# The forward-substitution steps of a delta-rule layer, moved from VectorE to GpSimd

## The chip, the cores and the metric

One core of one Trainium2 chip runs the whole program in one launch. The metric is the device time of that launch in microseconds, the median of several runs; lower is better.

In the rows of the profile PE is TensorE (PEld its weight loads), DVE is VectorE, ACT is ScalarE, POOL is GpSimd and SP is SyncE, whose queue issues most of the DMAs. L657 is line 657 of the kernel; a tile is named without its buffer number.

## The reference

One layer of a decoder trunk on 512 positions of width 2048, in float32:

```
h = RMSNorm(x);  z = h @ w_in
RWKV half (16 heads of 64): token shift of r, k, v and two small projections;
    w = exp(-exp(-softplus(-(w0 + tanh(wd) @ w_up)) - 0.5));  a = sigmoid(a0 + ad @ a_up)
    kk = normalized k * k_k;  k = k * (1 + (a - 1) * k_a)
    per head, over t:  S = S * w_t + (S @ -kk_t) (kk_t * a_t) + v_t k_t^T;  y_t = S @ r_t
    group norm per head, plus sum(r * k * r_k) * v, times silu(gate)
Pool half (4 groups of 256): trailing means over 2, 4, 8, 16 positions minus the token,
    a linear map per group, a scale, times silu(gate)
x = x + concat(halves) @ w_out
x = x + sigmoid(x @ w_pg + b_pg) * (p @ w_ple);  out = RMSNorm(x)
```

The recurrence over t is not run token by token. The kernel cuts the 512 positions into 8 chunks of 64. Inside a chunk the delta rule is a triangular system, whose inverse is needed; from chunk to chunk only the 64 x 64 state of a head is handed on.

## The kernel before

Every large product is split into three fp32r matmuls (high x high, high x low, low x high), so each weight chunk of 256 KB that the SP queue loads (`raw_*`) is cast on ScalarE (`whi_*`, L132) and its remainder is taken on VectorE (`wlo_*`, L133). Four buffers of each kind rotate.

The RWKV half is worked through in 8 pairs of heads, `j` = 0 to 7. For one pair: `prepare` makes the scaled keys and queries, `scores(j)` the triangular matrices `mt`, `invert(j)` inverts their 32 x 32 diagonal blocks by forward substitution, `gather(j)` builds the rest of the inverse `x1` from them, and `recur(j)` runs the 8 chunks. The work of neighbouring pairs overlaps: after the first chunk of `recur(j)` come `scores(j + 1)`, and the substitution of pair j + 1 runs during the later chunks of `recur(j)`. Between all these TensorE is fed with the matmuls of the input projection (`zk`, `zr`, `zv`, `zg` and the pool columns `zb`), which `pump` hands out a few at a time; the order on TensorE in this stage is the order of the program text (`keep_in_program_order`). On the other engines a scheduler sets the order when the program is built; each engine then works through its own queue strictly in that order, and so does SP.

A chunk `ch` of `recur` is a chain of hops, each with some 6 to 9 matmuls of the projection behind it:

- TensorE `py` reads the state `sbd`; VectorE forms `zs` (L787);
- TensorE `pu` multiplies by `x1`; ScalarE copies it to `uv` (L797);
- TensorE `ps` makes the state's update; VectorE forms the next state `sbd` in two halves. In chunk 0 that is L807, in the chunks 1 to 6 L809, which adds `s0p`;
- GpSimd forms `s0p`, the new state times the next chunk's decay, in two halves (L816). The next chunk's L809 reads it.

So `s0p_2` (made after chunk 2) is read by L809 of chunk 3, `s0p_3` by that of chunk 4, and so on up to `s0p_5`.

`invert(j)` is a generator of 31 steps of two instructions each: L657 multiplies a column of the result so far (`xw`) by a row of the matrix (`n`, loaded twice over from DRAM) into `tm`, and L661 adds `tm` to `xw`. Each reads what the one ahead of it wrote, so the 62 form one chain. The shapes run from 31 columns over 76 to 8 columns, 1560 columns over the 31 steps. Behind the last step SP writes `xw` to DRAM (`xd`, L665, four DMAs) and reads it back in another layout into `x1` (L672, four DMAs); VectorE transposes half of it (L734), and the matmuls `pq` use that.

Before the change the steps ran on VectorE, and inside `recur` they were tied to the hops: from the sixth hop on, each hop's end asked for two steps, to be issued behind the VectorE instruction that the hop had just issued (`lead`). For pair 0, whose `invert(0)` runs ahead of all recurrences, nothing was tied.

```
HC, HT, HX = (6, 9, 9), 130, 13
HS, HN = 5, 2                      # from which hop on, steps per hop
for _ in invert(0): pass           # pair 0
recur(j, invert(j + 1) if j + 1 < NJ else iter(()), between)
```

Of the kernel before, what the change touches and what calls it, by code (L numbers as in the profile page):

```python
# [13 lines left out]
ALU = mybir.AluOpType  # L14

P = 128
# [18 lines left out]
def trunk_kernel(ctx: ExitStack, tc: tile.TileContext, x, p, norm_g, w_in, mu, w0, w_up, a0, a_up,  # L35
                 k_k, k_a, r_k, ln_w, ln_b, w_pool, pool_scale, w_out, w_ple, w_pg, b_pg, final_g, out):
    nc = tc.nc
# [155 lines left out]
    n_ = 0  # L193
# [456 lines left out]
    def invert(j):  # L650
        nb = st_[j].pop("nb")
        xw = rw.tile([P, 8, 32], F32, name=f"xw{j}", tag="xw")
        tm = rw.tile([P, 8, 32], F32, name=f"tm{j}", tag="tm")
        for s in range(31):
            n_, w_ = s // 4 + 1, 31 - s
            xin = i32 if s == 0 else xw
            nc.vector.tensor_tensor(tm[:, 0:n_, 0:w_], xin[:, 0:n_, s:s + 1].to_broadcast([P, n_, w_]),  # L657
                                    nb[s // 16][:, s % 16:s % 16 + 1, s + 1:32].to_broadcast([P, n_, w_]), ALU.mult)
            if s == 0:
                nc.gpsimd.tensor_copy(xw, i32)  # L660
            nc.vector.tensor_tensor(xw[:, 0:n_, s + 1:32], xw[:, 0:n_, s + 1:32], tm[:, 0:n_, 0:w_], ALU.add)  # L661
            yield
        xd = dram.tile([2, 2, 8, 8, 4, 32], F32, name=f"xd{j}", tag="xd")
        for q in range(4):
            nc.sync.dma_start(out=xd[:, :, :, :, q, :].rearrange("a b u i c -> (a b u) i c"),  # L665
                              in_=xw[32 * q:32 * q + 32])
        x1 = rw.tile([P, 8, C], F32, name=f"x1{j}", tag="x1", bufs=2)
        nc.gpsimd.memset(x1, 0.0)
        for par in range(2):
            pb = 64 * (1 - par)  # L670
            for b in range(2):
                nc.sync.dma_start(out=x1[pb + 32 * b:pb + 32 * b + 32, :, 32 * b:32 * b + 32],  # L672
                                  in_=xd[par, b].rearrange("u i q c -> (i q) u c"))

        st_[j]["x1"] = x1
# [80 lines left out]
    def recur(j, work, between):  # L756
# [4 lines left out]
        lead = [None]  # L761


        def step():
            hop[0] += 1
            if hop[0] > HS:
                with tc.issue_after(lead[0].ins):
                    for _ in range(HN):
                        next(work, None)


        ysb = rw.tile([P, NT, P], F32, name=f"ysb{j}", tag="t", bufs=4)
# [1 line left out]
        for ch in range(NCH):  # L774
# [8 lines left out]
            if ch > 0:  # L783
                mm(py[:, sl], ar[:, q, 2 * par:2 * par + 2, :], cur, start=ch in (1, 4), stop=True,
                                 skip_group_check=True)
                with tc.high_priority(offset=HP):
                    lead[0] = nc.vector.tensor_tensor(zs[pb:pb + 64], py[pb:pb + 64, sl], mv[pb:pb + 64, q, :],  # L787
                                                      ALU.add)
                step()
                pump(HC1)  # L790
# [3 lines left out]
            for h in range(2):  # L794
                hc = slice(64 * h, 64 * h + 64)
                with tc.high_priority(offset=HP):
                    nc.scalar.copy(uv[pb:pb + 64, ch, hc], psu[hc, hc])  # L797
            step()
            pump(HC2)
            if ch < NCH - 1:  # L800
# [16 lines left out]
            if ch % 4 == 3:  # L817
# [10 lines left out]
                for pr in range(2):  # L828
                    yr = slice(64 * pr, 64 * pr + 64)
                    nc.scalar.copy(ysb[yr, q - 1:q + 1, :], py4[yr, pr::2, :])  # L830
            step()
            if ch == 0:
                between()
# [37 lines left out]
    HS, HN = 5, 2  # L871
# [12 lines left out]
    for _ in invert(0):  # L884
        pass
    pump(HT)
    gather(0)
    for j in range(NJ):
        def between():
            pump(H3 if j + 1 < NJ else HC[2])  # L890
            if j + 1 < NJ:
                scores(j + 1)
                pump_to(H2)

        if j + 1 == NJ:
            pn.append(rw.tile([P, NT, DPLE], F32, name="pn", tag="ar", bufs=2))
            for h in range(2):
                nc.scalar.dma_start(out=pn[0][:, 2 * h:2 * h + 2, :],
                                    in_=p[256 * h:256 * h + 256, :].rearrange("(t p) q -> p t q", p=P))
        if j + 1 < NJ:  # L900
            prepare(j + 1)
        recur(j, invert(j + 1) if j + 1 < NJ else iter(()), between)
        if j + 1 < NJ:
            gather(j + 1)
# [276 lines left out]
```

## Time and profile before

| | us |
|---|---|
| median of 3 runs | 1099.41 (1097.35 to 1099.85) |
| span of the profiled execution | 1095.9 |
| PE busy | 1070.8 (98%) |
| DVE busy | 708.2 (65%) |
| ACT busy | 448.3 (41%) |
| POOL busy | 76.9 (7%) |

The profiled execution's span runs from its first instruction to its last; its own time with what lies around the span is not listed apart, so the 3.5 us between the span and the median of the runs are taken as lying around it. "Busy" is the time in which an engine executes instructions of its own; a row of the time line gives the start in microseconds from the span's start, the duration, the engine, the line, the operation, what is written and read, and in square brackets the idle time ahead of it and what ended it. A row with x2 is two instructions that follow each other, its duration that of both together.

The first 37 us are the norm and the first transposes, from there to about 729 us run the input projection and the recurrences, and the rest is the output projection, the embedding and the last norm.

### The profile page before, as it was taken

Reading aid. Unit: us, or ns where it says so; the run is one execution under the profiler, and the core shown is the slowest. Engines: PE = TensorE matmul, PEld = TensorE weight load, DVE = VectorE, ACT = ScalarE, POOL = GpSimd, SP = SyncE. Lnnn points to the kernel's source line nnn. Section 1 sums busy time; section 2 is a strip of 40 time slices with the busy share of each in tenths; the row PEclk is TensorE's granted clock in tenths of the full one; section 3 lists DMA queues with packets and bytes.
Section 4 is the critical chain, followed back from the end, with each engine's and each line's share of the span. In section 5 each row is a group of like instructions: output and inputs, shape, how many; then the busy total and the mean of one; then the engine's idle time right before and its main releaser. Section 6 shows DMA issues by size and latency. Waiting matters only on the chain.

```text
span 1095.9 us, 17196 instructions
## 1 busy us (share of the span) xinstructions
PE 1070.8 (98%) x6060; PEld 877.6 (80%) x6060; DVE 708.2 (65%) x1835; ACT 448.3 (41%) x917; POOL 76.9 (7%) x180
## 2 busy tenths in 40 slices
PE   5999999999999999999999999999999999999996
PEld 4888878887788888788878788888888888888885
DVE  6687867878688679678886956454433424445366
ACT  7633535345335335353343344543222222233337
POOL 2100110110110110100101101000000000000000
PEclk9999999999999999999999999999999999999999
DMA  7433433332423333333334242775534438455534
GB/s 233 116 96 97 111 92 84 96 100 73 120 82 105 104 92 89 96 82 93 91 94 119 79 138 93 232 233 169 172 124 136 167 99 244 137 189 137 181 106 154
DMA packets 178486, 138.56 MB, mean 126 GB/s; under 512 B 34678, under 2 KB 139743, under 8 KB 178399
## 3 DMA queue, kind: packets, MB, share of 16 engines
q1 hardware_dynamic: 157694, 103.89, 32.1%
q10 hardware_dynamic: 20704, 33.56, 9.8%
q8 instruction: 48, 0.79, 0.3%
q14 instruction: 40, 0.32, 0.1%
HBM read 118.02 MB, written 18.87 MB: 125 GB/s over the span
## 4 chain that ended last, share of the span: by engine, by line
PE 86%; DVE 5%; DMA 4%; ACT 3%; issue 1%; SPq 0%; ACTq 0%; DVEq 0%
PE acc_o L157 16%; PE zb L157 14%; PE acc_g L157 14%; PE zv L157 8%; PE zk L157 7%; PE zg L157 7%; PE zr L157 7%; PE py L157 2%; PE pple L157 2%; PE pm L157 1%; PE pu L157 1%; DMA n<-nd 1%; PE pp L157 1%; DMA raw_g<-in_w_pg_dram 1%; PE ps L157 1%
## 5 line engine op out<-in xcount | busy, mean ns | idle before, releaser
L133 DVE TENSOR_TENSOR wlo_g<-raw_g,whi_g 128x512 fp32r<-128x512 f32 x84 | 57.0, 685 | 79.6 <-ACT whi_g L132 76.5
L157 PE MATMUL zb<-hhi,whi_b 128*128 128x512 f32 x256 | 107.0, 418 | 0.0
L133 DVE TENSOR_TENSOR wlo_o<-raw_o,whi_o 128x512 fp32r<-128x512 f32 x64 | 43.9, 690 | 91.4 <-ACT whi_o L132 91.4
L157 PE MATMUL zb<-hhi,wlo_b 128*128 128x512 f32 x256 | 100.5, 393 | 0.0
L157 PE MATMUL acc_o<-whi_o,ylo 128*128 128x512 f32 x256 | 100.2, 391 | 0.0
L157 PE MATMUL acc_o<-whi_o,yhi 128*128 128x512 f32 x256 | 99.9, 390 | 0.0
L157 PE MATMUL zb<-hlo,whi_b 128*128 128x512 f32 x256 | 99.9, 390 | 0.0
L157 PE MATMUL acc_o<-wlo_o,yhi 128*128 128x512 f32 x256 | 99.8, 390 | 0.0
L132 ACT CAST whi_g<-raw_g 128x512 fp32r<-128x512 f32 x84 | 51.9, 620 | 102.7 <-PE acc_g L157 55.4
L157 PE MATMUL acc_g<-whi_g,x2hi 128*128 128x512 f32 x208 | 81.3, 391 | 0.0
L157 PE MATMUL acc_g<-wlo_g,x2hi 128*128 128x512 f32 x208 | 80.9, 389 | 0.0
L157 PE MATMUL acc_g<-whi_g,x2lo 128*128 128x512 f32 x208 | 80.7, 389 | 0.0
L132 ACT CAST whi_o<-raw_o 128x512 fp32r<-128x512 f32 x64 | 39.9, 623 | 97.0 <-PE acc_o L157 96.7
L816 POOL TENSOR_SCALAR s0p<-sbd,pw 64x64 f32<-64x64 f32 x96 | 56.6, 589 | 322.8 <-DVE sbd L809 255.0
L132 ACT CAST whi_b<-raw_b 128x512 fp32r<-128x512 f32 x64 | 39.7, 621 | 86.5 <-PE zv L157 35.4
L133 DVE TENSOR_TENSOR wlo_b<-raw_b,whi_b 128x512 fp32r<-128x512 f32 x64 | 43.8, 685 | 34.2 <-ACT whi_b L132 32.9
L157 PEld LDWEIGHTS zb<-hhi,wlo_b 128*128 128x128 f32 x256 | 48.0, 188 | 11.1
L661 DVE TENSOR_TENSOR xw<-xw,tm 128x60 f32<-128x60 f32 (+24 forms) x248 | 52.1, 210 | 6.8
L157 PEld LDWEIGHTS acc_o<-wlo_o,yhi 128*128 128x128 f32 x256 | 48.1, 188 | 10.3 <-DVE wlo_o L133 0.4
L157 PEld LDWEIGHTS acc_o<-whi_o,yhi 128*128 128x128 f32 x256 | 48.1, 188 | 9.7
L157 PEld LDWEIGHTS acc_o<-whi_o,ylo 128*128 128x128 f32 x256 | 48.1, 188 | 9.8
L157 PEld LDWEIGHTS zb<-hhi,whi_b 128*128 128x128 f32 x256 | 48.2, 188 | 8.5
(285 smaller groups left out, 2550.0 us busy)
## 6 DMA issues: line engine op xcount, KB each, us to landing
raw_b<-in_w_in_dram SPq DMA_DIRECT2D x64, 256.0 KB
raw_o<-in_w_out_dram SPq DMA_DIRECT2D x64, 256.0 KB
raw_g<-in_w_pg_dram SPq DMA_DIRECT2D x64, 256.0 KB
raw_k<-in_w_in_dram SPq DMA_DIRECT2D x32, 256.0 KB
raw_r<-in_w_in_dram SPq DMA_DIRECT2D x32, 256.0 KB
raw_v<-in_w_in_dram SPq DMA_DIRECT2D x32, 256.0 KB
raw_g<-in_w_in_dram SPq DMA_DIRECT2D x32, 256.0 KB
n<-nd SPq DMA_DIRECT2D x16, 256.0 KB
```

What stands on the lines that cost most here:

```text
L132: nc.scalar.copy(hi, raw)
L133: nc.vector.tensor_tensor(lo, raw, hi.bitcast(F32), ALU.subtract)
L157: i = nc.tensor.matmul(*a, **k)
L661: nc.vector.tensor_tensor(xw[:, 0:n_, s + 1:32], xw[:, 0:n_, s + 1:32], tm[:, 0:n_, 0:w_], ALU.add)
L816: nc.gpsimd.tensor_scalar(s0p[hc, :], nxt[hc, hc], pcn[hc], None, ALU.mult)
```

## The change

The two instructions of a step are issued on GpSimd instead of on VectorE, for all eight pairs, and the tie to `lead` is taken away; from the sixth hop on, each hop still asks for two steps in the program text. The number of steps, their operands and all DMAs are the same.

```
         for s in range(31):
             n_, w_ = s // 4 + 1, 31 - s
             xin = i32 if s == 0 else xw
-            nc.vector.tensor_tensor(tm[:, 0:n_, 0:w_], xin[:, 0:n_, s:s + 1].to_broadcast([P, n_, w_]),
+            nc.gpsimd.tensor_tensor(tm[:, 0:n_, 0:w_], xin[:, 0:n_, s:s + 1].to_broadcast([P, n_, w_]),
                                     nb[s // 16][:, s % 16:s % 16 + 1, s + 1:32].to_broadcast([P, n_, w_]), ALU.mult)
             if s == 0:
                 nc.gpsimd.tensor_copy(xw, i32)
-            nc.vector.tensor_tensor(xw[:, 0:n_, s + 1:32], xw[:, 0:n_, s + 1:32], tm[:, 0:n_, 0:w_], ALU.add)
+            nc.gpsimd.tensor_tensor(xw[:, 0:n_, s + 1:32], xw[:, 0:n_, s + 1:32], tm[:, 0:n_, 0:w_], ALU.add)
             yield
...
         def step():
             hop[0] += 1
             if hop[0] > HS:
-                with tc.issue_after(lead[0].ins):
-                    for _ in range(HN):
-                        next(work, None)
+                for _ in range(HN):
+                    next(work, None)
```

GpSimd's queue in `recur(0)`, before: the copy that starts `xw` for pair 1, then the `s0p` of the six chunks, each in two halves, and nothing between them.

```order
L660 COPY xw_1862<-i_116 128x256
L816 TENSOR_SCALAR s0p_0_1694<-sbd_567,pw_836 64x64 x2
L816 TENSOR_SCALAR s0p_1_1836<-sbd_566,pw_836 64x64 x2
L816 TENSOR_SCALAR s0p_2_1908<-sbd_567,pw_836 64x64 x2
L816 TENSOR_SCALAR s0p_3_1985<-sbd_566,pw_836 64x64 x2
L816 TENSOR_SCALAR s0p_4_2069<-sbd_567,pw_836 64x64 x2
```

The same queue after (the line of `s0p` is now 815), at the place of `s0p_2`.

```order
L657 TENSOR_TENSOR tm_1863<-xw_1862,n_1_1764 128x5x14
L661 TENSOR_TENSOR xw_1862<-xw_1862,tm_1863 128x5x14
L815 TENSOR_SCALAR s0p_2_1908<-sbd_567,pw_836 64x64
L657 TENSOR_TENSOR tm_1863<-xw_1862,n_1_1764 128x5x13
L661 TENSOR_TENSOR xw_1862<-xw_1862,tm_1863 128x5x13
L815 TENSOR_SCALAR s0p_2_1908<-sbd_567,pw_836 64x64
L657 TENSOR_TENSOR tm_1863<-xw_1862,n_1_1764 128x5x12
L661 TENSOR_TENSOR xw_1862<-xw_1862,tm_1863 128x5x12
```

All 62 instructions of pair 1 now stand between `s0p_1` and `s0p_3`: 36 ahead of the first half of `s0p_2`, 2 between its halves, and 24 behind it. In `recur(6)` they are 36, 5 and 21; in `recur(1)` one step's instruction comes ahead of `s0p_1`, 2 between its halves, then 39, 2 and 18. The other recurrences are like one of these, within a few instructions.

SP's queue for pair 1, before: behind the last chunk of the `r` weights come all of `v` and `b`, and only then the first `xd`.

```order
L129 DMA raw_r_3_1300<-in_w_in_dram 128x4x128
L129 DMA raw_v_0_1306<-in_w_in_dram 128x4x128
L129 DMA raw_v_1_1324<-in_w_in_dram 128x4x128
L129 DMA raw_v_2_1330<-in_w_in_dram 128x4x128
L129 DMA raw_v_3_1348<-in_w_in_dram 128x4x128
L129 DMA raw_b_0_1354<-in_w_in_dram 128x4x128
L129 DMA raw_b_1_1376<-in_w_in_dram 128x4x128
L129 DMA raw_b_2_1382<-in_w_in_dram 128x4x128
L129 DMA raw_b_3_1400<-in_w_in_dram 128x4x128
L665 DMA xd_2253<-xw_1862 256x1x32 x2
```

And after: `xd`, which waits for the last step, stands directly behind the `r` weights, and the `v` weights stand behind it.

```order
L129 DMA raw_r_3_1300<-in_w_in_dram 128x4x128
L665 DMA xd_2253<-xw_1862 256x1x32
L129 DMA raw_v_0_1306<-in_w_in_dram 128x4x128
L665 DMA xd_2253<-xw_1862 256x1x32 x3
L129 DMA raw_v_1_1324<-in_w_in_dram 128x4x128
L672 DMA x_2258<-xd_2253 32x8x32 x2
L129 DMA raw_v_2_1330<-in_w_in_dram 128x4x128
L672 DMA x_2258<-xd_2253 32x8x32 x2
L129 DMA raw_v_3_1348<-in_w_in_dram 128x4x128
```

So the first `xd` of pair 1 has moved past eight weight loads, and the other pairs' likewise; that of pair 0 now stands ahead of the last `v` chunk and the first two `b` chunks. The order on TensorE is the same as before, and VectorE's queue is the old one without the steps but for some neighbours that change places.

More of the change, by code (lines that the diff above doesn't have):

```diff
@@ L656, in invert @@
             xin = i32 if s == 0 else xw
-            nc.vector.tensor_tensor(tm[:, 0:n_, 0:w_], xin[:, 0:n_, s:s + 1].to_broadcast([P, n_, w_]),
+            nc.gpsimd.tensor_tensor(tm[:, 0:n_, 0:w_], xin[:, 0:n_, s:s + 1].to_broadcast([P, n_, w_]),
                                     nb[s // 16][:, s % 16:s % 16 + 1, s + 1:32].to_broadcast([P, n_, w_]), ALU.mult)
@@ L660, in invert @@
                 nc.gpsimd.tensor_copy(xw, i32)
-            nc.vector.tensor_tensor(xw[:, 0:n_, s + 1:32], xw[:, 0:n_, s + 1:32], tm[:, 0:n_, 0:w_], ALU.add)
+            nc.gpsimd.tensor_tensor(xw[:, 0:n_, s + 1:32], xw[:, 0:n_, s + 1:32], tm[:, 0:n_, 0:w_], ALU.add)
             yield
@@ L766, in step @@
             if hop[0] > HS:
-                with tc.issue_after(lead[0].ins):
-                    for _ in range(HN):
-                        next(work, None)
+                for _ in range(HN):
+                    next(work, None)
         ysb = rw.tile([P, NT, P], F32, name=f"ysb{j}", tag="t", bufs=4)
```

## The prediction

> **What bounds the kernel now.** I read the engines' totals first, then the recurrences alone (135 to 656 us, `recur(0)` to `recur(6)` in seven stretches), then who waits there.
>
> ```profile
> PE 1070.8 (98%) x6060; PEld 877.6 (80%) x6060; DVE 708.2 (65%) x1835; ACT 448.3 (41%) x917; POOL 76.9 (7%) x180
> core 0: us, PE busy (x) PEld busy (x) DVE busy (x) ACT busy (x) POOL busy (x), PEclk, DMA share, GB/s
> sum 521.00, PE 517.65 PEld 420.76 DVE 407.35 ACT 216.38 POOL 58.14; mean PE 73.95 PEld 60.11 DVE 58.19 ACT 30.91 POOL 8.31
> PEld py L157 <- DVE sbd L809: 5.2, 9, 1.4
> ```
>
> TensorE bounds the kernel. In the 521 us of the recurrences it is idle for 521.00 - 517.65 = 3.4 us, although VectorE is busy for 407. So relieving VectorE can win 3.4 us there at most. Some of it is waiting for L809, the state, which is the chain that must not get longer: TensorE's order is fixed, and a late state stops everything behind it.
>
> **What the change removes.** The 496 instructions leave VectorE.
>
> ```profile
> L661 DVE TENSOR_TENSOR xw<-xw,tm 128x60 f32<-128x60 f32 (+24 forms) x248 | 52.1, 210 | 6.8
> ```
>
> With as many L657 that is about 13 us a pair. I cost the relief at nothing: it could show only as part of the 3.4 us, and the hops concerned get a longer wait below.
>
> **What one step's instruction takes on GpSimd.** The trace has no two-input operation there. These are the nearest rows, the first two from the groups by line, the others from the time line:
>
> ```profile
> L816 POOL TENSOR_SCALAR s0p<-sbd,pw 64x64 f32<-64x64 f32 x96 | 56.6, 589 | 322.8 <-DVE sbd L809 255.0 <-DVE sbd L807 63.3
> L77 POOL TENSOR_SCALAR_AFFINE_SELECT msk<-msk 64x64 f32<-64x64 f32 x6 | 1.2, 236 | 0.1
> 218.42 0.97 POOL L816 TENSOR_SCALAR s0p<-sbd,pw 64x64 f32<-64x64 f32 x2 [10.69 <-DVE sbd L809]
> 224.99 0.44 POOL L816 TENSOR_SCALAR s0p<-sbd,pw 64x64 f32<-64x64 f32 x1 [5.60 <-DVE sbd L809]
> 205.15 2.58 POOL L816 TENSOR_SCALAR s0p<-sbd,pw 64x64 f32<-64x64 f32 x2 [3.30 <-DVE sbd L807]
> 205.41 0.69 DVE L138 TENSOR_TENSOR kpl<-kp,kph 128x512 fp32r<-128x512 f32 x1
> 206.02 0.28 DVE L526 TENSOR_TENSOR as<-ar,as 64x128 fp32r<-64x128 f32 x1
> 206.22 0.68 DVE L133 TENSOR_TENSOR wlo_g<-raw_g,whi_g 128x512 fp32r<-128x512 f32 x1
> 206.82 0.68 DVE L417 TENSOR_TENSOR sw<-u 128x511 f32<-128x511 f32 x1
> ```
>
> An undisturbed `s0p` takes 0.44 us, and two take 0.97, so 0.53 from start to start: 0.09 lie between them. It reads a tensor of 64 columns and one value per partition. A step reads two tensors, of 1560 / 31 = 50 columns on average, and waits for its predecessor on the same engine. Low end: the one-input L77, 0.236 + 0.09, taken as 0.30 because shapes get small. High end: the mean `s0p`, disturbed ones included, 0.589 + 0.09, taken as 0.70. I take t = 0.50 from start to start, near the undisturbed `s0p`: fewer columns, one tensor more, some disturbance. A chain of 62 then takes 31 us, as long as the whole substitution inside a recurrence takes now; the trouble is what stands behind it.
>
> The disturbance is real: at 205.15 the second `s0p` ends only at 207.73, when four VectorE operations in a row that read SBUF twice are over. The Trainium skill, page "SBUF — State Buffer", section "Who interferes with whom", says that such a VectorE operation and a GpSimd operation that reads SBUF exclude each other for the whole instruction. By it each such `wlo` would stop the steps, which leads to the rival with the high end; these rows agree. The page "GPSIMD Engine Reference", section "Elementwise — side-by-side cycle accounting", gives 1.96 times VectorE's time for an add; 1.96 x 0.21 = 0.41 us, without the gap, would be an estimate of about 1186 us in all by the working below.
>
> **What stands behind the steps: the state.** GpSimd's queue is in order, and 62 steps now stand ahead of `s0p_3`, 36 to 41 of them ahead of `s0p_2`. The times of before, for the first and the last of the seven recurrences:
>
> ```profile
> 147.90 0.19 DVE L657 TENSOR_TENSOR tm<-i,n 128x31 f32<-128x31 f32 x1 [2.33 <-DMA n<-nd]
> 155.85 0.60 DVE L809 SCALAR_TENSOR_TENSOR sbd<-ps,pw,s0p 64x64 f32<-64x64 f32 x2 [0.31 <-PE ps L157]
> 162.87 0.60 DVE L809 SCALAR_TENSOR_TENSOR sbd<-ps,pw,s0p 64x64 f32<-64x64 f32 x2 [1.08 <-PE ps L157]
> 164.68 0.38 PE L157 MATMUL py<-sbd,ar 128*128 128x128 f32 x2
> 598.42 0.19 DVE L657 TENSOR_TENSOR tm<-i,n 128x31 f32<-128x31 f32 x1 [2.20 <-DMA n<-nd]
> 614.61 0.60 DVE L809 SCALAR_TENSOR_TENSOR sbd<-ps,pw,s0p 64x64 f32<-64x64 f32 x2
> 615.27 0.48 PE L157 MATMUL py<-sbd,ar 128*128 128x128 f32 x2
> ```
>
> The first step waits for `n` in both kernels, so it starts at 147.9. `s0p_2` is done 38 steps and its own two halves later, 147.9 + 19.0 + 1.0 = 167.9; L809 of chunk 3 ran at 155.85 and is now 12 us late. `s0p_3` is done after all 62 and four halves, 147.9 + 31.0 + 2.0 = 180.9; L809 of chunk 4 is 18 us late. In `recur(6)` 598.42 + 33.0 = 631.4 against 614.61: 16.8 us. From chunk 5 on GpSimd is free and nothing is added. The seven lie between these two, 17.5 us on average; TensorE's `py` follows L809's end by 1.2 us in the first and 0.1 in the last, some 0.5 of which is cover. Sum: 7 x 17.0 = 119 us. VectorE's queue waits with L809, so the `wlo` behind it are late too, but TensorE stands in the same place.
>
> **SP's queue.** `xd` now stands ahead of the `v` weights and waits for the last step.
>
> ```profile
> 175.19 2.08 PE zv L157 x9
> 594.60 5.98 DMA raw_b<-in_w_in_dram
> ```
>
> In `recur(0)` the last step ends at about 180, and the first `v` chunk can be issued half a microsecond later. A chunk on the chain of waits took 6.0 us to land, and cast and remainder take 1.3 more: ready at 188. TensorE wanted it at 175.2, which the late state moves to 192. So I cost it at nothing; if the state were on time, it would cost up to 13 us a pair instead. `x1` is read later still, and delayed alike.
>
> **Pair 0.** Nothing else runs on GpSimd, but the wait is open:
>
> ```profile
> 89.28 0.19 DVE L657 TENSOR_TENSOR tm<-i,n 128x31 f32<-128x31 f32 x1 [3.83 <-DMA n<-nd]
> 108.29 0.18 DVE L661 TENSOR_TENSOR xw<-xw,tm 128x8 f32<-128x8 f32 x1
> 113.63 1.90 SPq L672 DMA_DIRECT2D x<-xd  x4
> 116.19 4.10 PE zv L157 x18
> 117.56 0.89 DVE L734 STREAM_TRANSPOSE y<-x 32x256 f32<-32x256 f32 x2
> 118.48 3.35 DVE L572 RECIPROCAL kk<-kk 128x512 f32<-128x512 f32 x1
> 121.75 1.22 DVE L133 TENSOR_TENSOR wlo_b<-raw_b,whi_b 128x512 fp32r<-128x512 f32 x2
> ```
>
> 89.3 + 31 = 120.3 instead of 108.5, 12 us later. The four reads of `x1` are issued until 115.5, and the transposes follow at 117.56, so these have about 1 us to spare; behind them VectorE holds the `wlo_b` that TensorE needs at once. 11 us. The last `v` chunk, now behind two `xd`, would be ready at about 121.6 + 7.3 = 129 for the last twelve `zv` matmuls at 117.6: the same 11 us, at the same time, so counted once.
>
> **Sum.** 119 + 11 = 130 us on the profiled span of 1095.9: 1226, and with the 3.5 us between span and median 1229 us.
>
> **Rivals.**
> - *The clock falls as well.* TensorE stands still for about 12 and then 6 us in each recurrence. At the end of the trace, where it has nothing more to do, its granted clock halves:
>
> ```profile
> 1080.00:1087.00 7.00, 7.00 (x49) 6.43 (x47) 4.96 (x12) 5.11 (x10) 0.00 (x0) 1.00 0.48 173
> 1092.00:1095.90 3.90, 0.00 (x0) 0.00 (x0) 0.00 (x0) 0.00 (x0) 0.00 (x0) 0.50 0.59 213
> ```
>
>   That is within 5 us of the last matmuls. After the first stop the slow stretch hides in the second; after the second I allow 3 us a recurrence, 21 in all: 1250 us. Against it: the second stop is the shorter one. The Trainium skill, page "TensorE: Matmul & The Clock Gate", section "HAM oscillation — how this bites in real kernels", says that idle gaps over about 3.4 us bring the half clock back; the trace agrees on the halving.
> - *Steps at the low end*, 0.30: 62 x 0.30 + 2 = 20.6 after `n`, so L809 of chunk 4 is 5.6 us late in `recur(0)`, about 6 on average; 7 x 6 + 3 for pair 0 = 45: 1144 us.
> - *VectorE keeps GpSimd out*, steps at 0.70: 43.4 + 2 against 15.0 is 30 us a recurrence, 7 x 30 + 23 = 233: 1332 us. For it: the 2.58 us above. Against: while L809 waits, VectorE stands still and leaves GpSimd alone.
> - *Not slower.* The place is `s0p_2` in `recur(6)`: 41 steps and two halves must fit between 598.42 and L809 of chunk 3, some 8 us, which takes steps of 0.17 us or less. Then nothing is late and up to 3.4 us come back: 1096 us. Against it: even the one-input L77 takes 0.236.
>
> **How the numbers follow.** Forecast 0.50, clock 0.18, low end 0.18, high end 0.10, not slower 0.04. The likeliest is 1229. The range runs from 1150 to 1320: it leaves out the last case, under half of the low end (steps below 0.32) and about half of the high end, some 0.17. A change below 0.2%, 2.2 us, can't be told from none; by these cases faster has 0.02, same 0.02, slower 0.96.
>
> **What would show it.** Steps of 0.4 to 0.6 us from start to start on GpSimd; per recurrence two long waits of VectorE's L809 for GpSimd's `s0p`, in chunks 3 and 4, with TensorE's `py` behind them; TensorE's busy time nearly unchanged, some 17 us more idle in each recurrence, and the stages behind 729 us only shifted. The forecast is wrong if the steps overlap or take below 0.2 us, or if TensorE waits for `zv` rather than `py`.

## The result, and the profile after

| | median, us | ratio to before |
|---|---|---|
| before, beside the changed kernel | 1099.7 (1097.35 to 1100.93) | |
| after | 1194.9 (1192.6 to 1198.9) | 1.088 [1.086, 1.090] |

The change makes the kernel 8.8% slower, by 95 us. The forecast was 1229 us, the range 1150 to 1320. The profiled execution of after has a span of 1193.2 us, 97.3 more than before, and a mean granted clock of 0.963 against 0.998.

First the totals of the engines, then two of the seven recurrences (as stretches from 144 to 748 us; the third number from the end is the mean granted clock) and the sum of the seven:

```profile
PE 1091.2 (91%) x6060; PEld 892.7 (75%) x6060; DVE 618.8 (52%) x1339; ACT 448.0 (38%) x917; POOL 227.8 (19%) x676
219.00:305.00 86.00, 76.76 (x484) 62.40 (x483) 47.69 (x115) 32.05 (x70) 29.14 (x77) 0.94 0.30 81
653.00:748.00 95.00, 79.92 (x484) 64.49 (x483) 46.54 (x120) 27.32 (x61) 28.79 (x75) 0.91 0.31 87
sum 604.00, PE 532.63 PEld 430.97 DVE 327.09 ACT 213.48 POOL 190.88; mean PE 76.09 PEld 61.57 DVE 46.73 ACT 30.50 POOL 27.27
```

VectorE lost 89 us of work, and the kernel gained nothing by it. The recurrences went from 521 to 604 us in these stretches, which hold 3329 matmuls against 3357 before. Cut at the first state of each recurrence instead (129.30 to 656.45 us before, 141.00 to 755.25 us after, with 3401 and 3399 matmuls), they went from 527.2 to 614.3 us. Of these 87 us, 68 are TensorE standing still (71.4, before 3.4) and 19 are as many matmuls taking longer, at a mean granted clock of 0.91 to 0.96. Over the whole span TensorE is busy 20.4 us longer.

The groups by line of the steps and of `s0p`, and from the list of waits those of the state L808 (L809 before), of TensorE and of ScalarE (us in total, times, longest):

```profile
L661 POOL TENSOR_TENSOR xw<-xw,tm 128x60 f32<-128x60 f32 (+24 forms) x248 | 79.7, 322 | 19.2
L657 POOL TENSOR_TENSOR tm<-xw,n 128x60 f32<-128x60 f32 (+10 forms) x240 | 76.4, 318 | 18.3
DVE sbd L808 <- POOL s0p L815: 74.1, 25, 10.4
PE py L157 <- DVE sbd L808: 58.5, 10, 11.5
PE pbk L161 <- ACT sig L532: 10.6, 1, 10.6
```

A step's instruction takes 0.32 us on GpSimd, against 0.21 on VectorE. `py` waits 58.5 us for the state, and the state waits 74.1 us for `s0p`; the longest wait of `py`, 11.5 us in `recur(5)`, has another cause, shown further below. The time line of `recur(0)` shows the queue at work, here L808 of chunks 2, 3 and 4 and GpSimd's first and last step with the `s0p` around them:

```profile
160.90 0.60 DVE L808 SCALAR_TENSOR_TENSOR sbd<-ps,pw,s0p 64x64 f32<-64x64 f32 x2 [2.13 <-POOL tm L657]
173.78 0.28 DVE L808 SCALAR_TENSOR_TENSOR sbd<-ps,pw,s0p 64x64 f32<-64x64 f32 x1 [8.75 <-POOL s0p L815]
184.59 0.28 DVE L808 SCALAR_TENSOR_TENSOR sbd<-ps,pw,s0p 64x64 f32<-64x64 f32 x1 [6.21 <-POOL s0p L815]
159.37 0.24 POOL L657 TENSOR_TENSOR tm<-i,n 128x31 f32<-128x31 f32 x1 [3.05 <-DMA n<-nd]
173.31 0.43 POOL L815 TENSOR_SCALAR s0p<-sbd,pw 64x64 f32<-64x64 f32 x1
183.93 0.22 POOL L661 TENSOR_TENSOR xw<-xw,tm 128x8 f32<-128x8 f32 x1
184.12 2.33 POOL L815 TENSOR_SCALAR s0p<-sbd,pw 64x64 f32<-64x64 f32 x4
```

`s0p_2` starts behind 36 steps, at 173.31, and the state of chunk 3 follows at 173.78; `s0p_3` starts behind all 62, and the state of chunk 4 follows at 184.59.

### The profile page after: what moved, and what is told of

It reads as the page before. It is cut to its first block, busy times and chain, and to the rows that moved or that the text cites. A ratio compares the mean times of both kernels' runs of the same rounds, so it can differ in the third digit from the quotient of the medians.

```text
span 1193.2 us, 17185 instructions
## 1 busy us (share of the span) xinstructions
PE 1091.2 (91%) x6060; PEld 892.7 (75%) x6060; DVE 618.8 (52%) x1339; ACT 448.0 (38%) x917; POOL 227.8 (19%) x676
## 4 chain that ended last, share of the span: by engine, by line
PE 70%; POOL 13%; DMA 6%; issue 4%; ACT 3%; DVE 2%; SPq 1%; ACTq 0%; POOLq 0%; DVEq 0%
PE acc_o L157 15%; PE acc_g L157 14%; PE zb L157 13%; POOL xw L661 6%; POOL tm L657 6%; PE zv L157 6%; PE zg L157 5%; DMA n<-nd 5%; PE zr L157 4%; PE pple L157 2%; PE zk L157 2%; PE py L157 1%; PE pm L157 1%; POOL s0p L815 1%; PE pu L157 1%
## 5 line engine op out<-in xcount | busy, mean ns | idle before, releaser
L815 POOL TENSOR_SCALAR s0p<-sbd,pw 64x64 f32<-64x64 f32 x96 | 52.4, 546 | 185.5 <-DVE sbd L808 114.9
L808 DVE SCALAR_TENSOR_TENSOR sbd<-ps,pw,s0p 64x64 f32<-64x64 f32 x96 | 27.1, 282 | 113.0 <-POOL s0p L815 74.1
L661 POOL TENSOR_TENSOR xw<-xw,tm 128x60 f32<-128x60 f32 (+24 forms) x248 | 79.7, 322 | 19.2
L657 POOL TENSOR_TENSOR tm<-xw,n 128x60 f32<-128x60 f32 (+10 forms) x240 | 76.4, 318 | 18.3
L157 PE MATMUL py<-sbd,ar 128*128 128x128 f32 x112 | 24.9, 306 | 58.6 <-DVE sbd L808 58.5
L157 PEld LDWEIGHTS py<-sbd,ar 128*128 128x128 f32 x112 | 21.4, 203 | 67.2 <-DVE sbd L808 63.8
L133 DVE TENSOR_TENSOR wlo_v<-raw_v,whi_v 128x512 fp32r<-128x512 f32 x32 | 22.4, 702 | 72.6 <-ACT whi_v L132 70.3
```

What stands on the lines that cost most here:

```text
L133: nc.vector.tensor_tensor(lo, raw, hi.bitcast(F32), ALU.subtract)
L157: i = nc.tensor.matmul(*a, **k)
L657: nc.gpsimd.tensor_tensor(tm[:, 0:n_, 0:w_], xin[:, 0:n_, s:s + 1].to_broadcast([P, n_, w_]), nb[s // 16][:, s % 16:s % 16 + 1, s + 1:32]. ...
L661: nc.gpsimd.tensor_tensor(xw[:, 0:n_, s + 1:32], xw[:, 0:n_, s + 1:32], tm[:, 0:n_, 0:w_], ALU.add)
L808: lead[0] = nc.vector.scalar_tensor_tensor(nxt[hc, hc], pss[hc, hc], pcc[hc], s0p[hc, :], ALU.mult, ALU.add)
L815: nc.gpsimd.tensor_scalar(s0p[hc, :], nxt[hc, hc], pcn[hc], None, ALU.mult)
```

## The experiments

Each kernel is the changed one with the edit shown, unless said otherwise. The first table compares all of them: how much later than before the first state of `recur(0)` (L807) starts, which is what pair 0 loses; what the seven recurrences then add until the first state of `recur(7)`, both read from the time lines; and the time, with its ratio to runs of before taken beside it (medians from 1097.6 to 1099.7 us). In `recur(7)` no further pair is inverted.

| kernel | pair 0, us | seven recurrences, us | median, us | ratio to before |
|---|---|---|---|---|
| after | 11.7 | 87.1 | 1194.9 | 1.088 [1.086, 1.090] |
| s0p_on_vector | 12.3 | 85.1 | 1194.0 | 1.089 [1.086, 1.092] |
| xd_behind_weights | 12.1 | 82.8 | 1189.9 | 1.083 [1.081, 1.086] |
| own_n_alone | 13.9 | 78.8 | 1186.6 | 1.079 [1.077, 1.082] |
| pair0_xd_behind_v | 6.9 | 86.6 | 1191.7 | 1.086 [1.083, 1.089] |
| both_blocks_out | 13.2 | 27.3 | 1135.2 | 1.033 [1.030, 1.035] |
| both_out_pair0_vector | 0.3 | 25.9 | 1123.2 | 1.023 [1.021, 1.025] |
| three_blocks_out | 0.4 | -3.3 | 1093.0 | 0.995 [0.994, 0.996] |
| untied_on_vector (of before) | 0.2 | 30.7 | 1131.3 | 1.031 [1.030, 1.033] |
| tied_to_s0p | 11.9 | 27.5 | 1131.4 | 1.032 [1.029, 1.034] |
| tied_pair0_vector | 0.4 | 24.1 | 1118.8 | 1.019 [1.017, 1.021] |
| tied_own_n | 0.3 | 2.0 | 1098.5 | 1.000 [0.999, 1.002] |
| before_own_n (of before) | -0.4 | 0.4 | 1096.0 | 0.998 [0.997, 0.999] |

**s0p_on_vector: the state taken out of GpSimd's queue.**

```
-nc.gpsimd.tensor_scalar(s0p[hc, :], nxt[hc, hc], pcn[hc], None, ALU.mult)
+nc.vector.tensor_scalar(s0p[hc, :], nxt[hc, hc], pcn[hc], None, ALU.mult)
```

> The changed kernel with s0p made on VectorE, so that nothing of the state's chain stands in GpSimd's queue; the steps, their place and SP's queue stay as in the changed kernel. Queue theory (s0p stands behind the steps): VectorE's waits for s0p, 74 us of the changed kernel, go; what is left over 1100 is pair 0, 12 us, and perhaps weights that xd holds up, up to 5 us a recurrence: 1110 to 1146 us. Weights theory (xd ahead of the v weights is what costs): little comes back, 1175 to 1195 us. Slow theory (GpSimd is too slow or kept out of SBUF, whatever stands behind it): the inverse is late all the same, 1160 us or more.

Nothing came back. The list of waits shows what took the state's place; then ScalarE's and SP's rows in `recur(0)`:

```profile
PE ps L157 <- ACT uv L796: 38.9, 7, 9.1
PE pu L157 <- DVE zs L786: 18.0, 2, 17.6
ACT whi_v L132 <- DMA raw_v<-in_w_in_dram: 65.2, 8, 14.4
188.08 0.62 ACT L132 CAST whi_v<-raw_v 128x512 fp32r<-128x512 f32 x1 [9.76 <-DMA raw_v<-in_w_in_dram]
189.12 0.42 ACT L796 COPY uv<-pu 64x64 f32<-64x64 f32 x2
184.21 0.61 SPq L665 DMA_DIRECT2D xd<-xw  x1
184.92 0.54 SPq L129 DMA_DIRECT2D raw_v<-in_w_in_dram  x1
```

The state is on time up to chunk 4. Then SP's queue, where `xd` stands ahead of the `v` weights, holds these until the last step is done (184.21). ScalarE's cast `whi_v` waits for the weights, and `uv`, which the recurrence needs, stands behind it in ScalarE's queue. So this second block reaches the recurrence through a copy behind a cast, not through the weights' own matmuls. The first three recurrences lose 10.9, 11.2 and 9.7 us to it, about what they lose with the late state; the 85 us of all seven hold some of a third block, found below. In `recur(6)` the late `xd` acts another way: VectorE's transposes wait 18.0 us for the reads of `x` and stand ahead of `zs`, for which `pu` waits 17.6 us.

**xd_behind_weights: SP's queue put back, the state left on GpSimd.** A dependency that orders but doesn't wait keeps the `xd` of pairs 1 to 7 behind the weights:

```
+d_ = nc.sync.dma_start(out=xd...)
+if state[0] is not None:
+    tc.add_manual_dep(d_.ins, state[0].ins.name, mybir.DependencyInfo(
+        mybir.DependencyClass.NoSync, mybir.DependencyReason.DATA))
```

> The changed kernel with an ordering edge that puts the xd of pairs 1 to 7 behind the hop in which they stand in the program, so that SP issues the v and b weights ahead of them as before the change; GpSimd's queue and pair 0 as in the changed kernel. Queue theory: 1185 to 1197 us, the state's waits stay at some 74 us. Weights theory: about 1110 us.

```profile
DVE sbd L814 <- POOL s0p L821: 76.2, 26, 10.4
PE py L157 <- DVE sbd L814: 60.5, 12, 10.5
```

Only some 5 us came back, and the wait of the state for `s0p` stands as it was: the first three recurrences lose 11.4, 11.4 and 10.1 us. The 5 us lie in `recur(6)`, which loses 13.2 us here and 20.1 in the changed kernel: the transposes of pair 7 no longer stand ahead of `zs` there. The two blocks lie side by side, and either is enough.

**both_blocks_out: the two edits together.**

> The changed kernel with both edits at once: s0p on VectorE, and the four xd copies of pairs 1 to 7 put behind the recurrence's last weight loads in SP's queue. Theory (two in-order queues, each enough by itself to lose about 10 us a recurrence): nothing that TensorE wants stands behind the steps any more, so the seven recurrences lose 0 to 1 us each and only pair 0's 11.7 us remain: 1097.6 + 12 = 1110 us (1103 to 1118); no wait of py for the state above 2 us, none of whi_v for raw_v above 3 us in the recurrences. Rival 1 (there is a third block, or the steps disturb VectorE over SBUF): the recurrences still lose 4 us or more each: 1138 or above. Rival 2 (the granted clock by itself is what costs, whatever stands still): the clock stays at 0.96 and the time at 1140 or above though no wait is long.

Of the 87 us in the recurrences 60 came back, but 27 stayed, against 0 to 7 expected. The theory of two queues missed, and the rival of a third block was nearer, though not with its even 4 us for each. They sit in three recurrences: `recur(0)` to `recur(2)` lose nothing, `recur(3)` 7 us, `recur(4)` 8 and `recur(5)` 12. The next kernel shows the same without pair 0.

**both_out_pair0_vector: pair 0's steps back on VectorE as well.** The edit takes `eng = nc.vector if j == 0 else nc.gpsimd` for the two instructions of a step.

> As both_blocks_out, and the steps of pair 0 on VectorE as before the change; the steps of pairs 1 to 7 stay on GpSimd. Theory: all three losses are gone, 1097.6 us within 4 us, ratio 0.997 to 1.004; a gain of at most 3 us from VectorE's relief. Rival (a third block): 1125 us or above, as for both_blocks_out less 12.

Pair 0's 13 us came back in full; the 26 us of `recur(3)` to `recur(5)` stayed, as the rival had it. The time lines of ScalarE and VectorE in `recur(3)`, then ScalarE in `recur(5)`:

```profile
385.19 0.72 ACT L557 ACTIVATE kk<-sk,prm 128x512 f32<-128x512 f32 x1 [5.99 <-POOL tm L660]
385.81 0.60 ACT L132 CAST whi_v<-raw_v 128x512 fp32r<-128x512 f32 x1
386.45 0.69 DVE L133 TENSOR_TENSOR wlo_v<-raw_v,whi_v 128x512 fp32r<-128x512 f32 x1 [7.62 <-ACT whi_v L132]
387.06 0.59 DVE L815 SCALAR_TENSOR_TENSOR sbd<-ps,pw,s0p 64x64 f32<-64x64 f32 x2
547.70 0.72 ACT L557 ACTIVATE kk<-sk,prm 128x512 f32<-128x512 f32 x1 [11.34 <-POOL tm L660]
```

This is a third block, which I had not seen. `n[0]`, which the first 16 steps read, lies in the buffer in which ScalarE forms a later pair's `kk`. So L557 waits for GpSimd's steps to have read it: 6.0 us in `recur(3)`, 11.3 in `recur(5)`. Behind `kk` in ScalarE's queue stands a cast `whi_v`; on VectorE the remainder `wlo_v` waits for that, and behind it in VectorE's queue stands the state of chunk 3, 6.5 us later behind that of chunk 2 than before. In `recur(0)` to `recur(2)` the same wait is 3.9 us at most and nothing comes of it.

**three_blocks_out: a buffer of its own for n[0] in addition.** Room for it comes from `x1`, which gets one buffer instead of two.

```
-t_ = rw.tile([P, 16, 32], F32, name=f"n32{j}_{i}", tag=("kk", "kp")[i])
+t_ = rw.tile([P, 16, 32], F32, name=f"n32{j}_{i}", tag=("n0", "kp")[i])
-x1 = rw.tile([P, 8, C], F32, name=f"x1{j}", tag="x1", bufs=2)
+x1 = rw.tile([P, 8, C], F32, name=f"x1{j}", tag="x1", bufs=1)
```

> As both_out_pair0_vector (steps of pairs 1 to 7 on GpSimd, s0p and pair 0 on VectorE, xd late in SP's queue), and n[0], which the first 16 steps read, has a buffer of its own instead of the buffer of kk; to make room x1 has one buffer instead of two. Theory (a third in-order queue: ScalarE's kk of the next pair overwrites the buffer of n[0] and so waits up to 11 us for the steps, with whi_v behind it in ScalarE's queue): recur(3), (4) and (5) get back their 6.5, 7.4 and 13 us, 1123 - 26 = 1097 us, ratio 0.996 to 1.002, granted clock above 0.99. Rival (the delay of recur(3) to (5) has another cause, as disturbance by GpSimd over SBUF or the late xd reads themselves): above 1115 us.

```profile
PE 1068.6 (98%) x6060; PEld 879.3 (81%) x6060; DVE 655.8 (60%) x1497; ACT 448.4 (41%) x917; POOL 171.1 (16%) x518
ACT kk L557 <- DVE sk L370: 10.7, 4, 5.9
PEld py L157 <- DVE sbd L815: 1.1, 2, 0.6
```

All of it came back, and 5 us more: 1093.0 us, 0.5% faster than before [0.4, 0.6], at a mean granted clock of 0.997. `kk` no longer waits for GpSimd, and the weight loads of `py` wait 1.1 us in the recurrences (135 to 660 us) where they waited 5.2 before. The steps of seven pairs run on GpSimd here and take as long as in the changed kernel (25.5 to 30.0 us a pair, there 24.7 to 26.9), so it was not their length that cost, but what stood behind them in three queues.

**before_own_n: is the gain the buffer's?** The kernel before, with the same two lines on `n[0]` and `x1`.

> The kernel before with nothing but the own buffer for n[0] (x1 with one buffer); steps and s0p where they were before. Theory (three_blocks_out gains its 5 us, 2.9 of them in the recurrences, because VectorE has no steps ahead of L809, so that py's nine waits for it are gone): no gain here, 1098.4 us, ratio 0.998 to 1.002, and py still waits some 5 us in all for L809. Rival (the gain comes from kk's own buffer: ScalarE's kk waits less for VectorE): 1093 to 1095 us, as three_blocks_out.

```profile
PEld py L157 <- DVE sbd L809: 5.3, 8, 1.6
```

Neither theory quite: the buffer alone gives 0.19% [0.10, 0.28], some 2 us, and leaves the waits for L809. Against it, three_blocks_out is at 0.995 / 0.998 = 0.997, some 3 us (with the two intervals, 1.5 to 5) for all else that it changes. The steps away from VectorE are the likely part, since `py`'s waits for the state fall from 5.3 to 1.1 us; no run moves them alone.

**own_n_alone: the third block taken out of the changed kernel by itself.** The same two lines.

> The changed kernel with nothing else but the own buffer for n[0] (x1 with one buffer). Theory (three queues, each enough by itself): the state is late behind the steps in GpSimd's queue and the v weights behind xd in SP's, so nothing comes back: 1190 to 1197 us. Rival (kk's wait is the main block): 1170 or below.

```profile
DVE sbd L808 <- POOL s0p L815: 100.9, 30, 11.1
```

Some 8 us came back, a little more than expected; the state waits for `s0p` 101 us in all, where it waited 74. In `recur(5)`, where the changed kernel's state stands behind `kk`, it waits 9.2 us for `s0p` here. So the third block lies mostly side by side with the first.

**pair0_xd_behind_v: the way by which pair 0 loses.** Only pair 0's `xd` is put behind the last `v` chunk.

```
+after = newest[-2] if j == 0 else None      # the last v load issued
+with (tc.issue_after(after.ins) if after is not None else ExitStack()):
     nc.sync.dma_start(out=xd...)
```

In the changed kernel, SP's, ScalarE's and TensorE's rows there:

```profile
113.88 1.32 SPq L665 DMA_DIRECT2D xd<-xw  x2
115.31 0.54 SPq L129 DMA_DIRECT2D raw_v<-in_w_in_dram  x1
118.48 0.62 ACT L132 CAST whi_v<-raw_v 128x512 fp32r<-128x512 f32 x1 [14.38 <-DMA raw_v<-in_w_in_dram]
121.00 0.68 ACT L532 ACTIVATE sig<-pu,dprm 128x512 f32<-128x512 f32 x1
121.73 1.12 PE L161 MATMUL pbk<-ident,bk 128*128 128x128 f32 x4 [10.60 <-ACT sig L532]
```

> The changed kernel, but the four xd copies of pair 0 stand behind the last v weights in SP's queue; the steps of pair 0 stay on GpSimd, the recurrences stay as in the changed kernel. Theory (pair 0 loses its time by the way SP -> last raw_v -> ScalarE's cast whi_v -> sig behind it in ScalarE's queue -> pbk): that way is free, and what is left is the transposes, 5.4 us late since the steps end at 113.9 instead of 108.5: 6 of 11.7 us come back, 1195 - 6 = 1189 us (1186 to 1191), and pbk's wait of 10.6 us for sig goes. Rival (the prediction's first way, transposes with wlo_b behind them, costs the same by itself): no gain, 1194 to 1196 us.

By the time line 4.8 of pair 0's 11.7 us came back, near the 6 expected, and the wait of `pbk` is gone. In its place `pq` waits for the transposes and `pu` for `x`:

```profile
PE pq L159 <- DVE y L738: 3.3, 1, 3.3
PE pu L159 <- ACT x L756: 1.9, 1, 1.9
```

The time, 1191.7 us, agrees but can't be told from the changed kernel's by its interval. So pair 0 loses by both ways, and the longer one is SP, weights, cast, `sig`, `pbk`.

**untied_on_vector: the other half of the change alone.** The steps stay on VectorE and only the tie to the hops goes.

```
-with tc.issue_after(lead[0].ins):
-    for _ in range(HN):
-        next(work, None)
+for _ in range(HN):
+    next(work, None)
```

> The other half of the change alone: the steps stay on VectorE but are not tied to the hops. Queue theory: a chain of 62 at about 0.25 us is only 15 us, VectorE's queue gets no more than some 16 to 20 of them between two states, 4 to 5 us of the 6 to 7 between them: 1097 to 1108 us. Weights theory: xd moves up in SP's queue by about four loads here too, so some of the loss shows, 1120 us or more. Slow theory: 1100 us.

```profile
PEld pu L157 <- DVE zs L786: 32.3, 21, 3.7
```

I expected 10 us of loss at most, and it lost 34 us (3.1%), 3.4 to 5.7 us a recurrence: untied, the steps stand in groups of up to 15 ahead of `zs` or the state in VectorE's queue, with the tie in groups of at most 12, mostly 8 and 4. The theory of the weights had named such a time too, but no cast of `v` waits for its weights in this trace. So the tie was worth 34 us where the steps ran on VectorE.

**tied_to_s0p: the tie kept, on GpSimd.** `lead` is the newest `s0p`, so at most 12 of the steps' instructions stand between two `s0p`, and `xd` falls behind more of the weights.

```
-for _ in range(HN):
-    next(work, None)
+with tc.issue_after(lead[0].ins):
+    for _ in range(HN):
+        next(work, None)
-nc.gpsimd.tensor_scalar(s0p[hc, :], nxt[hc, hc], pcn[hc], None, ALU.mult)
+lead[0] = nc.gpsimd.tensor_scalar(s0p[hc, :], nxt[hc, hc], pcn[hc], None, ALU.mult)
```

> Steps on GpSimd, but each hop's two steps are tied behind the newest s0p, which puts at most 12 instructions between two s0p, and xd back behind most weights. Queue theory: 12 x 0.41 is 5 us of the 6 to 7 between two states, so no state waits; the last 17 steps end some 7 us after s0p_5, about when x1 is needed: 1108 to 1120 us, of which pair 0 is 12. Slow theory: the chain of 62 still takes its 25 us and the port is as busy, so most of the loss stays, 1160 us or more. Weights theory: also about 1110, xd being late again; the first two kernels tell that apart.

Sixty of the 87 us came back; 12 of pair 0 and 27 in the recurrences stayed, so the time is 11 us above the range expected.

**tied_pair0_vector and tied_own_n** take out these two in turn: pair 0's steps on VectorE, then `n[0]` in its own buffer besides.

> As tied_to_s0p (steps on GpSimd, tied behind the newest s0p, so that at most 12 of them stand between two s0p), and the steps of pair 0 on VectorE. Theory: pair 0's 11.4 us come back, the rest stays: 1131.4 - 11.5 = 1120 us (1116 to 1123). Rival (the recurrences' small losses there come from the late pair 0 and move with it): 1105 or below.

> As tied_pair0_vector (steps on GpSimd in groups behind each s0p, pair 0 on VectorE), and n[0] in a buffer of its own. Theory: the waits of ps for ScalarE's uv of 3 to 4 us in recur(2) to (5) go with kk's waits, 16 us less: 1119 - 16 = 1103 us (1099 to 1108); what is left is the seventh recurrence (transposes ahead of the state, 7 us). Rival (the small waits come from the GpSimd state being late by a few steps): 1114 or above.

Pair 0's edit gave back 12.6 us by the medians, and the buffer 20.3 more, where 16 were expected, which puts this kernel level with before. Some 5 us of loss are left in `recur(6)`. In tied_pair0_vector ScalarE's `kk` waited for the steps here too, and `uv` behind it:

```profile
ACT kk L557 <- POOL tm L658: 24.8, 6, 6.8
```

## Why the prediction was right, and where it was off

**The mechanism holds, for six of the seven recurrences.** GpSimd works its queue in order, `s0p` stands behind 36 and 62 steps, and `py` waits for the state: the two waits stand in chunks 3 and 4 of `recur(0)`, as forecast. The state waits long for `s0p` in both chunks in `recur(0)`, `recur(2)` and `recur(6)` (8.8 and 6.2 us, 9.1 and 4.4, 10.2 and 3.7), in one of them in `recur(1)`, `recur(3)` and `recur(4)` (10.4, 3.3 and 5.5 us), and not at all in `recur(5)`. Behind these waits `py` stands for 47 of TensorE's 71.4 us (58.5 less the 11.5 of `recur(5)`).

**The mis-sized term is the lateness of the state**, 17 us a recurrence. In `recur(0)` chunk 3 came out 6.2 us later than pair 0's shift explains (12 forecast) and chunk 4 3.8 more, 10.0 in all (18 forecast). Two sizes were off. The steps took 0.40 us from start to start there, 24.8 for the 62 (25.7 on average over the eight pairs), where I took 0.50 and 31.0: they came out as mean durations of 0.32 and a gap of about 0.08, and a disturbance only now and then. And the state waits for half an `s0p`: its first half starts 0.04 us after the first half of `s0p` ends, 0.44 us behind the last step, where I charged four halves, 2.0 us. 17.0 - 6.2 - 1.6 = 9.2, and `recur(0)` lost 9.3.

**The rest of the recurrences' sum** is 87 - 7 x 9.2 = 23 us. About 8 are in `recur(6)`, where the changed order put the transposes of pair 7 on VectorE ahead of `zs`, and so ahead of the state of chunk 5; the prediction said that nothing is added from chunk 5 on, and this was overlooked in the order:

```profile
713.12 0.44 DVE L734 STREAM_TRANSPOSE y<-x 32x256 f32<-32x256 f32 x1 [6.14 <-DMA x<-xd]
713.59 0.28 DVE L786 TENSOR_TENSOR zs<-py,mv 64x128 f32<-64x128 f32 x1
719.10 0.28 DVE L808 SCALAR_TENSOR_TENSOR sbd<-ps,pw,s0p 64x64 f32<-64x64 f32 x1 [3.65 <-PE ps L157]
```

From chunk 4 to chunk 5 the state's delay against before grows by 8.1 us. In xd_behind_weights, where the transposes do not stand there, it grows by 2.1.

The other 15 lie in `recur(1)` and `recur(3)` to `recur(6)`, 2 to 4 us each. TensorE's longer busy time, 19 us in the seven, is of that size, but 2.4 us of it lie inside the 9.3 of `recur(0)`; that it makes up these 15 was not shown.

**Some of the nearness is luck.** Where the third block is out (own_n_alone), `py` waits 62.5 us for the state, about half of the 119 charged. In the changed kernel 18 us of stops from the third block, 5 from the transposes and 19 of slower matmuls, which the sum did not hold, made up part of the difference.

**The clock rival came about too.** I forecast TensorE's busy time as nearly unchanged; it rose by 20.4 us, close to the 21 that this rival allowed, and the stretches of the recurrences were granted 0.91 to 0.96 on average. The kernels without stops have 0.995 and more. The way was another than the rival's: it put the slow matmuls behind the second stop of a recurrence, but behind the second stops of `recur(0)`, `recur(2)` and `recur(6)` (1.6 to 1.8 us) there were none, and behind the first there were. So the low steps (a rival, 1144 us) and the clock (a rival, 1250 us) both happened in part, and 1195 lies between.

**SP's queue, costed at nothing,** was right in the sum: with it put back, 5 us of 95 returned, and those from the transposes. The clause beside it, up to 13 us a pair if the state were on time, is borne out by s0p_on_vector: 9.7 to 11.2 us in each of the first three recurrences, where the third block alone costs nothing.

**Pair 0: 11 us forecast, 11.7 measured,** but by two errors that cancel. The steps ended 5.4 us later than before, not 12, so the transposes alone would have cost about 5 (6.9 remain in pair0_xd_behind_v). The way through the last `v` chunk made it 11.7, and not because `zv` lacked the weights: `sig` stood behind the cast in ScalarE's queue.

**What the prediction did not have** is ScalarE's queue, with `kk` behind the steps by a shared buffer. In the changed kernel it alone stops `recur(5)`, and in `recur(4)` `ps` waits 6.3 us for the `uv` that stands behind `kk`. ScalarE's, VectorE's and TensorE's rows in `recur(5)`; the second half of the state of chunk 2 stands behind this `wlo_v`:

```profile
600.63 0.72 ACT L557 ACTIVATE kk<-sk,prm 128x512 f32<-128x512 f32 x1 [13.09 <-POOL tm L657]
601.90 0.69 DVE L133 TENSOR_TENSOR wlo_v<-raw_v,whi_v 128x512 fp32r<-128x512 f32 x1 [12.12 <-ACT whi_v L132]
602.97 0.80 PE L157 MATMUL py<-sbd,ar 128*128 128x128 f32 x2 [11.49 <-DVE sbd L808]
```

Taking it out of the changed kernel returned only 8 us, because `s0p` is late there all the same, and 26 us once the other two blocks were gone.

**VectorE's relief, costed at nothing** with a bound of 3.4 us, is worth about 3 us if nothing else in three_blocks_out gained, and shows only when all three blocks are out.

## What to carry to other kernels

A chain of small operations that is moved to an idle engine should be judged by who queues behind it: on that engine, on the DMA queue behind the transfer that waits for its end, and on any engine that next writes a buffer which it reads. Three such blocks lay side by side here, and taking out any one returned 1 to 8 of 95 us, taking out all three, and pair 0's, returned everything, so a fix that gains nothing by itself doesn't show that its cause was wrong. A cast in an in-order queue passes its wait to whatever small copy stands behind it, so look for the wait at the operation behind, not at the weights' own reader.

## What was not expected of the hardware

- GpSimd's two-input operation on small tiles in float32 costs 1.5 times VectorE's (0.32 against 0.21 us on average): undisturbed 0.21 to 0.22 us for 8 columns and 0.32 to 0.35 for 76, with about 0.08 us between an operation and the one that needs its result. This is why t was too high. The Trainium skill, page "GPSIMD Engine Reference", section "Elementwise — side-by-side cycle accounting", has 1.96 times for an add of large tiles; the runs here have 1.5, and the estimate of 0.41 us that the prediction drew from it came near only because it left out the gap. GpSimd's rows in `recur(0)` of after:

```profile
168.66 0.32 POOL L657 TENSOR_TENSOR tm<-xw,n 128x76 f32<-128x76 f32 x1
169.06 0.35 POOL L661 TENSOR_TENSOR xw<-xw,tm 128x76 f32<-128x76 f32 x1
183.65 0.21 POOL L657 TENSOR_TENSOR tm<-xw,n 128x8 f32<-128x8 f32 x1
```

- Disturbance was exact but rare. Of the 62 steps in that chain four took 0.60 to 0.77 us instead of about 0.30, and each of the four lies under one of the four `wlo`, and ends 0.1 to 0.2 us after it. The `sg` at 162.25, which reads `zg` from PSUM, stretched none:

```profile
161.59 0.74 POOL L661 TENSOR_TENSOR xw<-xw,tm 128x28 f32<-128x28 f32 x1
162.40 0.28 POOL L657 TENSOR_TENSOR tm<-xw,n 128x54 f32<-128x54 f32 x1
161.53 0.69 DVE L133 TENSOR_TENSOR wlo_k<-raw_k,whi_k 128x512 fp32r<-128x512 f32 x1
162.25 0.69 DVE L374 SCALAR_TENSOR_TENSOR sg<-sg,zg 128x512 f32<-128x512 f32 x1
```

  The rule of the Trainium skill that the prediction cited for this, page "SBUF — State Buffer", section "Who interferes with whom", agrees. It cost little: the four make up some 1.8 of the 24.8 us, and in the other chains 4 to 9 steps were stretched. In three_blocks_out, where VectorE does not stand still, six of the seven chains take 25.5 to 26.1 us, so its standing still is not what kept the cost low.
- Behind a stop TensorE ran at half its clock for some microseconds, and the mean hides this. In the changed kernel each of the ten stops of 2.8 to 11.5 us (from 121 us to the end of the recurrences) was followed by 2.7 to 6.2 us in which the 128x512 matmuls started every 0.43 us instead of every 0.23; behind the three stops of 1.6 to 1.8 us they did not. Over a recurrence that makes a mean granted clock of 0.91 to 0.96, and over the seven 19 us more of TensorE's busy time, on top of the 68 us of standing still. The stretches behind the stop of `recur(5)`, with the granted clock third from the end:

```profile
603.00:606.40 3.40, 3.40 (x10) 2.82 (x11) 0.88 (x2) 0.00 (x0) 2.93 (x9) 0.50 0.27 77
606.80:609.00 2.20, 2.20 (x13) 1.74 (x11) 0.43 (x1) 1.00 (x3) 1.78 (x6) 1.00 0.03 7
```
